# Strided attention on one core: the load of the values as one transfer, or as three on two queues

## The chip, the cores and the metric

The kernel runs on one core of a Trainium2 chip. The metric is the device time of one execution in microseconds (us). Before the change the median of three runs is 127.71 us (127.59 to 128.22).

## What is computed

Q, K and V have the shape 8 x 12 x 1024 x 64 (batch, heads, sequence, dimension) in float32. Each query attends to every 64th key, so to 16 keys per head:

```python
attend_positions = np.arange(0, seq, stride)            # 16 positions
k = K[:, :, attend_positions, :]
v = V[:, :, attend_positions, :]
scores = np.einsum('bhqd,bhkd->bhqk', q, k) * scale
weights = np.exp(scores - np.max(scores, axis=-1, keepdims=True))
weights = weights / (np.sum(weights, axis=-1, keepdims=True) + 1e-10)
result[:, :, i, :] = np.einsum('bhqk,bhkd->bhqd', weights, v)[:, :, 0, :]
```

All of Q is read (25.2 MB) and a result of the same size is written. Of K and of V only 1536 rows of 64 numbers are read, 256 bytes each and far apart, 384 KB for each of the two.

## The kernel before, in words

The 96 heads are worked off in 24 groups of four heads. A group's queries are one load of 1 MB (L33, through the helper `_copy`, on the queue of the SyncE engine), its result is one store of 1 MB on the same queue. There are ten buffers for queries and eight for results.

At the start SyncE issues, in this order: the load of all keys (L106), the query load of group 0, the load of all values (L108), and the query loads of groups 1 to 9. After that, each pass of the loop over the groups issues the store of group g and then the query load of group g + 10, as long as there are groups left. The loads of the first two groups are laid out in 128 rows of 8 KB, the others in 32 rows of 32 KB; a store has rows of 8 KB as far as the DMA engines see it.

The order of the instructions on each engine is written out by hand (`manual_schedule`): every engine works through its list in that order, and waits stand where data are needed.

GpSimd (POOL) begins with the identity matrix (L121, L122), four copies that make `perm_v` from it (L129), and then waits for `s_sel`, which VectorE (DVE) makes from the identity (L136), to fill `v_all` and `mask` (L140, L141). Then come copies of keys into `k_t` (L159), its halves of the casts of the queries of groups 0 and 1 (L196), and the cast of the values to bf16 (`v_bf`, L294), the first instruction that reads the loaded values. Behind `v_bf` TensorE (PE) spreads the values over the partitions (L171), VectorE copies that to `v_rep` (L175), and GpSimd multiplies it with the mask (`v_all`, L184): this is the right side of the matmuls that make the outputs (L255).

Per group: ScalarE (ACT) and GpSimd each cast one half of the queries (L195, L196), VectorE transposes them in 32 x 32 blocks (L212), TensorE makes the scores (L221), ScalarE takes the exponential (L233), TensorE makes the outputs and the sums of weights in three pieces (L255), VectorE takes the reciprocals (L263) and multiplies two of the pieces by them (L265), while the third is copied by ScalarE (L269) and multiplied by GpSimd (L270). Then the group is stored.

Of the kernel before, what the change touches and what calls it, by code (L numbers as in the profile page):

```python
# [17 lines left out]
def _ap_with(ap: bass.AP, new_ap, extra_offset: int = 0) -> bass.AP:  # L18
    return dataclasses.replace(
        ap, ap=[list(p) for p in new_ap], offset=ap.offset + extra_offset  # L20
    )
# [27 lines left out]
def kernel(  # L49
# [8 lines left out]
    nc = tc.nc  # L58

    B, H, S, D = Q.shape  # L60
# [24 lines left out]
    v_raw = const.tile([P, NC, D], FP32, name="v_raw")  # L85
# [5 lines left out]
    kv_src = [[stride * D, P], [2 * HG * SD, NC], [1, D]]  # L91
# [6 lines left out]
    def load(g):  # L98
        qn[g] = qn_bufs[g % QBUFS]
        n = P if g < 2 else 32  # L100
        loaded[g] = _copy(nc, qn[g], _ap_with(Q, [[HG * SD // n, n], [1, HG * SD // n]], g * HG * SD))
        if g >= QBUFS:
            for earlier in (loaded[g - QBUFS], *cast_by[g - QBUFS]):
                implied(loaded[g], earlier, "the store before it has waited for both casts")

    nc.sync.dma_start(k_raw, _ap_with(K, kv_src))  # L106
    load(0)
    nc.sync.dma_start(v_raw, _ap_with(V, kv_src))  # L108
    for g in range(1, QBUFS):
        load(g)  # L110

# [172 lines left out]
    first, rest = slice(0, 4), slice(4, NC)  # L284
# [76 lines left out]
```

## Time and profile before

| what | value |
|---|---|
| median of three runs | 127.71 us (127.59 to 128.22) |
| the profiled execution: its time | 128.23 us |
| its span (first to last instruction) | 126.4 us |
| busy PE / DVE / ACT / POOL | 65.1 / 85.4 / 82.8 / 78.7 us |
| DMA packets, data moved | 7910, 51.19 MB, 405 GB/s over the span |
| of them under 512 B | 3872 |
| load of the values: issue on SyncE, time to landing | 2.00 us, 6.5 us |
| first reader of the values, `v_bf` on POOL | starts at 12.10 us |
| first store issued | 21.21 us |

The page of a profile lists the engines' busy times, the DMA queues with their packets and the share of the time of sixteen DMA engines that these took, and the chain of work that ended last. Other views of the same trace are the table of stretches (busy time of each engine, and share of the DMA engines, between two times), the timeline of one engine, and the waits of one tile. Times in them are microseconds from the start of the span. The trace also records each DMA packet with its queue, size, start and duration, and each mark by which a DMA engine reports its part of a transfer as landed; the records do not name the engine.

A transfer is cut into runs of consecutive bytes, which the trace shows as packets: the keys and the values together are 3072 packets of 256 bytes on SyncE's queue (q1), queries and results are packets of 8 KB and 32 KB. Every transfer of this kernel ends with sixteen marks, one for each DMA engine.

### The profile page before, as it was taken

How to read it: one execution, taken by the hardware profiler on the slowest of the kernel's cores; microseconds unless marked ns; L12 is line 12 of the kernel's file. 1: busy time of each engine (PE TensorE's matmuls, PEld its weight loads, DVE VectorE, ACT ScalarE, POOL GpSimd, SP SyncE). 2: the span in 40 equal slices, each digit the busy share in tenths (PEclk: the TensorE clock that was granted, in tenths of full speed). 3: DMA queues.
4: the chain of work that ended last, by engine and by line, in shares of the span. 5: the costliest groups of instructions: out<-in, count | busy, mean ns of one | idle time of the engine just before them, and what ended most of it. 6: DMA issues, size and time to landing. Idle time of an engine off the chain costs nothing.

```text
span 126.4 us, 1091 instructions
## 1 busy us (share of the span) xinstructions
PE 65.1 (52%) x292; PEld 28.6 (23%) x292; DVE 85.4 (68%) x151; ACT 82.8 (66%) x111; POOL 78.7 (62%) x89
## 2 busy tenths in 40 slices
PE   0005379446666655866666656657794486430000
PEld 0001132212322223333333332212321223200000
DVE  5931672959698979799999998955955956750000
ACT  4172809794989999969898988477486496620000
POOL 4084347763858688969898999566666756453000
PEclk9999999996899998599999999975569959955555
DMA  2999999989998998989989999989989899999991
GB/s 63 381 357 454 487 404 425 498 332 397 438 482 358 482 459 337 513 355 423 474 371 430 461 394 441 477 365 469 435 378 503 345 428 423 428 425 425 425 410 44
DMA packets 7910, 51.19 MB, mean 405 GB/s; under 512 B 3872, under 2 KB 3872, under 8 KB 3872
## 3 DMA queue, kind: packets, MB, share of 16 engines
q1 hardware_dynamic: 7904, 51.12, 96.9%
q8 instruction: 2, 0.03, 0.1%
q14 instruction: 4, 0.03, 0.1%
HBM read 25.95 MB, written 25.17 MB: 404 GB/s over the span
## 4 chain that ended last, share of the span: by engine, by line
DMA 50%; DVE 12%; ACT 10%; POOL 7%; PE 6%; issue 3%; SPq 2%; POOLq 1%; DVEq 0%
DMA qn<-in_Q_dram 50%; DVE out_sb L265 6%; ACT out_sb L269 4%; POOL out_sb L270 4%; PE o_ps L255 3%; DVE qt L212 3%; ACT qb L195 2%; POOL qb L196 2%; ACT w_all L233 2%; PE sc L221 2%; DVE rec L263 2%; ACT k_t L159 1%; POOLq L356 1%; SPq L33 1%; DVE v_rep L175 1%
## 5 line engine op out<-in xcount | busy, mean ns | idle before, releaser
L255 PE MATMUL o_ps<-v_all,w_all 128*128 128x260 bf16 x192 | 37.6, 310 | 35.8 <-DVE out_sb L265 26.1
L270 POOL TENSOR_TENSOR out_sb<-out_sb,rec 128x768 f32<-128x768 f32 x24 | 35.3, 1472 | 19.6 <-ACT out_sb L269 19.1
L265 DVE TENSOR_TENSOR out_sb<-o_ps,rec 128x768 f32<-128x768 f32 (+1 forms) x48 | 39.6, 824 | 1.6
L212 DVE STREAM_TRANSPOSE qt<-qb 128x1024 int32<-128x1024 int32 x24 | 29.4, 1226 | 13.9 <-POOL qb L196 13.9
L233 ACT ACTIVATE w_all<-sc 64x512 bf16<-64x512 f32 x48 | 35.3, 736 | 3.5 <-PE sc L221 3.0
L221 PE MATMUL sc<-qt,k_t 128*128 128x512 bf16 x96 | 32.0, 467 | 9.9 <-DVE qt L212 9.9
L255 PEld LDWEIGHTS <-w_all 128*128 128x128 bf16 x192 | 17.4, 106 | 60.5 <-DVE out_sb L265 33.7
L196 POOL CAST qb<-qn 128x1024 bf16<-128x1024 f32 x24 | 24.9, 1038 | 9.7 <-ACT qb L195 7.8
L195 ACT CAST qb<-qn 128x1024 bf16<-128x1024 f32 x24 | 25.0, 1046 | 8.9 <-DMA qn<-in_Q_dram 8.6
L269 ACT COPY out_sb<-o_ps 128x768 f32<-128x768 f32 x24 | 19.2, 799 | 13.3 <-DVE rec L263 12.9
L263 DVE RECIPROCAL rec<-o_ps 128x12 f32<-128x12 f32 (+1 forms) x72 | 15.1, 209 | 4.2 <-PE o_ps L255 3.7
L184 POOL TENSOR_TENSOR v_all<-mask,v_rep 128x256 bf16<-128x256 bf16 x24 | 16.1, 672 | 1.9 <-DVE v_rep L175 1.9
L221 PEld LDWEIGHTS <-k_t 128*128 128x128 bf16 x96 | 10.8, 113 | 20.2 <-POOL k_t L159 7.5
L159 ACT COPY k_t<-k_r 32x256 bf16<-32x256 bf16 (+1 forms) x12 | 4.4, 366 | 1.5 <-DVE k_r L150 1.3
L175 DVE CAST v_rep<-o_ps 128x768 bf16<-128x768 f32 x2 | 1.9, 956 | 4.4 <-PE o_ps L171 4.4
L133 DVE MEMSET k_t<- 128x3456 uint32 x1 | 2.9, 2938 | 1.5 <-PEq L342 1.5
L149 ACT CAST k_bf<-k_raw 128x256 bf16<-128x256 f32 (+1 forms) x2 | 1.0, 512 | 2.7 <-DMA k_raw<-in_K_dram 2.7
L140 POOL COPY v_all<-s_sel 128x12 bf16<-128x12 bf16 x1 | 0.2, 194 | 4.1 <-DVE s_sel L136 4.1
L171 PE MATMUL o_ps<-v_bf,perm_v 128*128 128x384 bf16 x4 | 1.3, 417 | 1.5 <-POOL v_bf L294 1.2
L149 ACT ACT_TABLE_LOAD x1 | 1.3, 1283 | 0.7 <-PEq L342 0.7
L150 DVE STREAM_TRANSPOSE k_r<-k_bf 128x128 int32<-128x128 int32 (+1 forms) x2 | 0.7, 370 | 1.4 <-ACT k_bf L149 1.4
L134 DVE MEMSET w_all<- 128x1536 uint32 x1 | 1.3, 1338 | 0.3 <-issue 0.3
(12 smaller groups left out, 4.6 us busy)
## 6 DMA issues: line engine op xcount, KB each, us to landing
qn<-in_Q_dram SPq DMA_DIRECT2D x24, 1024.0 KB, 15.3
out_dram<-out_sb SPq DMA_DIRECT2D x24, 1024.0 KB, 15.4
k_raw<-in_K_dram SPq DMA_DIRECT2D x1, 384.0 KB, 4.0
v_raw<-in_V_dram SPq DMA_DIRECT2D x1, 384.0 KB, 6.5
```

Of the source, the lines that this page charges most:

```text
L159: op(k_t[dst : dst + 32, 2 * part.start + c : 2 * part.stop : 2, :, col : col + NK], k_r[src : src + 32, part].rearrange("p n (a k f) -> p ...
L184: masked[g] = nc.gpsimd.tensor_tensor(out=vb[g][:, 0 : 4 * D].rearrange("p (s d) -> p s d", s=4), in0=mask, in1=v_rep[:, g // 2, g % 2].un ...
L195: late = nc.scalar.copy(qb[g][:, half:], qn[g][:, half:])
L196: early = nc.gpsimd.tensor_copy(out=qb[g][:, 0:half], in_=qn[g][:, 0:half])
L212: turned = nc.vector.transpose(qt[g].bitcast(I32), qb[g].bitcast(I32))
L221: nc.tensor.matmul(sc, lhsT=k_t[:, g, f, NK * (1 - e) : NK * (1 - e) + P], rhs=_ap_with(q, [q.ap[0], [D, 8], [16 * D, 2], [2, 32]], extra_ ...
L233: raised[g].append(nc.scalar.activation(out=_ap_with(wa, [wa.ap[0], [P, 8], [1, 2], [2, 32]], extra_offset=64 * a), in_=sc[64 * a : 64 * a ...
L255: nc.tensor.matmul(ps[:, i, 0 : 4 * D + 4], lhsT=wt[g][:, i0 + i], rhs=vb[g], start=True, stop=True,)
L263: nc.vector.reciprocal(r, ps[:, 0:n, 4 * D : 4 * D + 4])
L265: timed = nc.vector.tensor_tensor(out=to, in0=o, in1=by, op=ALU.mult)
L269: copied = nc.scalar.copy(to, o)
L270: scaled[g] = nc.gpsimd.tensor_tensor(out=to, in0=to, in1=by, op=ALU.mult)
```

## The change

The single load of the values (128 rows, one for each partition, each with 12 runs of 256 bytes) becomes three: rows 0 to 4 and rows 5 to 125 on the queue of GpSimd, and rows 126 and 127 on that of SyncE, there in the old place between the first two query loads. The two on GpSimd stand ahead of all its other instructions of the kernel. `v_bf` now waits for three transfers. The order of all other instructions on every engine is as before.

```diff
     nc.sync.dma_start(k_raw, _ap_with(K, kv_src))
     load(0)
-    nc.sync.dma_start(v_raw, _ap_with(V, kv_src))
+    def value_load(queue, first, rows):
+        queue.dma_start(
+            v_raw[first : first + rows],
+            _ap_with(V, [[stride * D, rows], *kv_src[1:]], first * stride * D),
+        )
+
+    value_load(nc.gpsimd, 0, 5)
+    value_load(nc.gpsimd, 5, 121)
+    value_load(nc.sync, 126, 2)
     for g in range(1, QBUFS):
         load(g)
```

## The prediction

> **What bounds the kernel now.** I read the DMA queues first, then the table of stretches, then the timelines of SP and POOL around the transfer that is changed, and last the trace's records of single DMA packets, which no view prints.
>
> The queues, on the page:
>
> ```profile
> q1 hardware_dynamic: 7904, 51.12, 96.9%
> q8 instruction: 2, 0.03, 0.1%
> q14 instruction: 4, 0.03, 0.1%
> HBM read 25.95 MB, written 25.17 MB: 404 GB/s over the span
> ```
>
> Packets, MB, and the share of 16 DMA engines' whole span: SP's queue keeps the sixteen engines busy 96.9% of 126.4 us, while the busiest compute engine has 68%. The table of stretches (columns: stretch, length, busy us and instructions of PE, PEld, DVE, ACT and POOL, PE clock, DMA share, GB/s) says when they are not busy:
>
> ```profile
> 3.00:31.00 28.00, 12.52 (x44) 5.17 (x45) 17.04 (x27) 15.55 (x23) 14.67 (x20) 0.97 1.03 414
> 31.00:50.00 19.00, 11.77 (x61) 5.38 (x60) 16.25 (x30) 18.31 (x28) 14.21 (x14) 0.95 1.01 427
> 75.00:101.00 26.00, 16.73 (x72) 6.87 (x71) 19.37 (x37) 16.95 (x22) 17.79 (x17) 0.80 1.01 426
> 115.00:123.00 8.00, 0.00 (x0) 0.00 (x0) 0.00 (x0) 0.00 (x0) 0.00 (x0) 0.50 1.01 424
> 123.00:124.00 1.00, 0.00 (x0) 0.00 (x0) 0.00 (x0) 0.00 (x0) 0.00 (x0) 0.50 0.36 148
> 124.00:125.00 1.00, 0.00 (x0) 0.00 (x0) 0.00 (x0) 0.00 (x0) 0.00 (x0) 0.50 0.14 57
> ```
>
> From 3 to 123 us all sixteen are full; compute is over by 115. Then the share falls to 0.36 and 0.14: **most engines are done and a few are not**. The sixteen completion marks of the last store show it: ten at 123.44 to 123.80 us, three at 124.03, 124.18 and 124.22, three at 125.09, 125.17 and 125.54. The span ends on the last one. An even share would have ended at about 124.0 (mean of the sixteen), so at most some 1.5 us can be won by sharing the packets out otherwise.
>
> Why are three late? The records carry no engine number, but on a full engine a 256 B packet follows the one before after 14 ns, an 8 KB packet after 307, so most can be strung into sixteen chains. Two of the three last chains lose 1.08 us at 48.0 and 1.01 us at 85.1, just behind the two 16 KB packets of q8 (47.0 and 84.1 us). Chains hit by an 8 KB packet of q14 lose about 0.3 us. The rest are short delays of single packets. So part of the lateness belongs to the engines that fetch instructions, and part is chance.
>
> **The change, part by part.** The time of this execution is 128.23 us: the span of 126.42 and 1.81 around it. The median of the runs shown is 127.71 (127.59 to 128.22), so the profiled one is the slow end, 0.4% above; I carry the ratio over to the median.
>
> *Packets of V per engine.* Before, 128 rows of 12 runs of 256 B on sixteen engines: 96 packets each, from 6.28 to 7.64 us on the first, 1.36 us, or 14 ns a packet. If the change's "5 and 11" holds and the two transfers take different engines, five engines get 1 row (12 packets) and eleven get 11 rows (132). Two engines get another 12 packets for SP's 2 rows; I take them to be among the five, otherwise two of the eleven are 0.17 us later. The five save 84 x 14 ns = **1.18 us** (1.01 with the extra row), the eleven pay 36 x 14 ns = **0.50 us**. All transfers behind V on an engine move by as much, since every engine is full from there to 123 us. Total work is unchanged. Completion marks cost 9 ns each: nothing.
>
> *The sum, if the three late engines are among the five:* the last goes from 125.54 to 124.36 (or 124.53), and what is late next are the eleven: the latest of the others, 124.22 + 0.50 = 124.72. The end moves by 125.54 - 124.72 = 0.82: 128.23 - 0.82 = 127.41 us, -0.64%, which on the median is **126.9**. With fewer hiccups among the eleven (123.80 + 0.50 = 124.30; then the end is the 124.53 of above) it is -1.01, 126.7; with a hiccup of 0.3 us (such as a q14 fetch) on one of them, -0.5, 127.2.
>
> *Issue on SP.* Three things of SP's start are touched:
>
> ```profile
> 0.74 0.43 SPq L106 DMA_DIRECT2D k_raw<-in_K_dram  x1
> 1.23 0.73 SPq L33 DMA_DIRECT2D qn<-in_Q_dram  x1
> 2.00 0.58 SPq L108 DMA_DIRECT2D v_raw<-in_V_dram  x1
> 21.21 0.63 SPq L33 DMA_DIRECT2D out_dram<-out_sb  x1
> 27.95 0.59 SPq L33 DMA_DIRECT2D out_dram<-out_sb  x1
> 33.18 0.59 SPq L33 DMA_DIRECT2D out_dram<-out_sb  x1
> ```
>
> The 2-row transfer keeps an issue slot between the first and second Q load: 0.43 to 0.73 us by these rows instead of 0.58, hidden behind 2.4 us of packets per load already queued. First data come 1.1 us after the K issue starts, at 1.84 us, and K stays first: no change.
>
> *Issue on POOL.* Two issues go ahead of everything POOL does:
>
> ```profile
> 0.73 0.21 POOL L121 MEMSET identity<- 128x128 bf16 x1 [0.29 <-POOLq L342]
> 1.01 0.29 POOL L122 TENSOR_SCALAR_AFFINE_SELECT identity<-identity 128x128 bf16<-128x128 bf16 x1
> 1.37 0.76 POOL L129 COPY perm_v<-identity 128x64 bf16<-128x64 bf16 x4
> 6.28 0.19 POOL L140 COPY v_all<-s_sel 128x12 bf16<-128x12 bf16 x1 [4.15 <-DVE s_sel L136]
> ```
>
> No row shows what an issue costs on POOL. Behind the two wait the identity (DVE's s_sel at 5.99 needs it, ready at 1.30: 4.7 us to spare), perm_v, and then the 4.15 us in which POOL waits anyway. Call the cost of both G. Lower bound: as SP, 2 x 0.43 = 0.9 us. Upper bound, if GpSimd writes 1512 runs one by one at the pace of its slowest row per element (L270, 1472 ns for 768): 2.9 us for one list, 5.8 if sources and destinations are two lists done in turn. I take 3, nearer to the one list. Up to 4.15 it is free.
>
> *Arrival of V.* L294 needs all three transfers; behind it on POOL are both value products, and behind those the first outputs. It runs at 12.10 while V has landed at 8.5: 3.6 us to spare. And the start as a whole has cover: store 0 is issued at 21.21, its data could flow at 22.3, but the engines are on the ten first Q loads until 30.2. Stores 1 and 2 have 6.0 and 5.6 us by the same count. So the delay D of the first outputs costs nothing up to 5.6 us (V landing by 17.7, or G up to 9.7), and D - 5.6 beyond.
>
> **A rule against it.** The trace prices V by which engines carry it, not by its total. The Trainium skill ("DMA: Bandwidth & Descriptors", section "Rules for kernel authors") says of two transfers to disjoint partition halves not to bother: they spread over the same sixteen engines, and one 128-partition transfer is to be used. By that rule the sum would be zero, 127.7.
>
> **The rivals.**
> *B, the late engines are not the five.* The trace does not show which engines the 5 rows fall on. If the last one is among the eleven it ends at 125.54 + 0.50: 128.73, or 128.2 on the median, +0.4%. For it: lateness is partly chance, and eleven of sixteen engines pay. Against: two of the three follow instruction fetches, so the same engines would be late each time.
> *C, the split isn't what it says.* If the 121 rows go to all sixteen engines in eights, each has 96 packets again, give or take a row (0.17 us): 127.7 (127.5 to 127.9). Then no engine takes much over 96 runs in the after trace. The Trainium skill (same page, section "Why a DMA increments its semaphore by 16 and not by 1") has both: the largest divisor up to 16, so 5 and 11, and an exception in which some direct GpSimd copies get sixteen engines with the rows rounded up. No trace here shows which.
> *D, V comes late.* On an engine, packets of another queue are taken between packets of a store (the fetches above do so in the middle of one). If the 132 runs of V take turns singly with Q's packets, they get 16 turns beside the 8 KB packets of the first two loads (5.1 us) and 16 beside the 32 KB packets of the other eight (1.23 us each, 19.8 us), and finish when those run out, at about 30. Then L294 waits 18 us more, D - 5.6 = 12.6, and the time is 140.8 in the profile's count (140 on the median). If sixteen runs go at a turn, 9 turns at most 1.45 us each end by 17, and it costs nothing. It decides at 17.7 us. A G of over 9.7 us has the same effect; at 12 us it costs 2.3.
>
> **How the numbers follow.** A 0.53 (126.3 to 127.3; a twentieth of the total within 0.5%), B 0.14 (mostly within), C 0.09 (within), D 0.24 (128.5 to 141, of it 0.07 up to 129; not more in all, since 9.7 lies above my upper bound for G, and turns of single runs are the extreme). A difference of 0.5%, 0.64 us, is about what a measurement of this kernel can tell from none. Faster 0.48, same 0.25, slower 0.27. The range 126.2 to 129.0 takes in A, B, C and the small cases of D; left out are the rest of D (0.17) and a little below (0.03).
>
> **What would show it.** Right: the sixteen marks of the last store lie closer, with the end set by an engine with 132 V packets; the DMA share in the second before last is higher; span near 125.6. Step by step: chains with 12 and 132 runs of 256 B besides K's; L294 before 17.7 us; store 2 issued before 38.8; no drop of the DMA share near 30 us. A stretch near 30 to 40 us with a share under 0.9 means D; marks as wide as before with all 0.5 later means B.

## The result, and the profile after

The changed kernel takes **130.21 us** (median of six runs, 130.00 to 130.36) where the kernel before takes 127.96 (127.59 to 128.35, six runs beside it): a ratio of 1.0175 (1.0149 to 1.0200), 2.25 us slower. The forecast was 126.9 us; the time lies above the range. The profiled execution took 130.16 us with a span of 128.3, to be set against 128.23 and 126.4 before.

The queues of the changed kernel, from the page:

```profile
q1 hardware_dynamic: 6378, 50.73, 95.4%
q0 software_dynamic: 192, 0.39, 1.1%
q8 instruction: 2, 0.03, 0.1%
q14 instruction: 5, 0.03, 0.1%
HBM read 25.95 MB, written 25.17 MB: 398 GB/s over the span
```

The bytes are the same and go at 398 GB/s instead of 404. The new queue q0 is GpSimd's. Its 192 packets are taken apart below. The table of stretches, cut as in the prediction and with the start cut finer (columns as there):

```profile
3.00:7.00 4.00, 0.00 (x0) 0.00 (x0) 3.16 (x4) 0.93 (x3) 2.30 (x10) 1.00 0.99 288
7.00:9.50 2.50, 0.00 (x0) 0.10 (x1) 0.00 (x0) 0.07 (x1) 0.45 (x2) 1.00 1.06 354
```

```profile
31.00:50.00 19.00, 11.13 (x55) 5.32 (x56) 16.95 (x32) 16.74 (x26) 13.32 (x14) 0.91 1.00 423
75.00:101.00 26.00, 15.38 (x79) 7.04 (x78) 20.81 (x39) 20.23 (x26) 19.83 (x20) 0.94 1.00 422
```

```profile
124.00:125.00 1.00, 0.00 (x0) 0.00 (x0) 0.00 (x0) 0.00 (x0) 0.00 (x0) 0.50 0.90 377
125.00:126.00 1.00, 0.00 (x0) 0.00 (x0) 0.00 (x0) 0.00 (x0) 0.00 (x0) 0.50 0.35 147
126.00:127.00 1.00, 0.00 (x0) 0.00 (x0) 0.00 (x0) 0.00 (x0) 0.00 (x0) 0.50 0.14 57
```

At the end the same falling stair stands as before, 0.35 and 0.14, only two us later: the engines are no more level than they were. From 31 to 101 us the engines are as full as before and move about as much. At the start, though, the share stays at 0.99 and 1.06 while 288 and 354 GB/s are moved. The same two stretches in the kernel before:

```profile
3.00:7.00 4.00, 0.00 (x0) 0.00 (x0) 3.16 (x4) 0.93 (x3) 0.66 (x3) 1.00 1.04 351
7.00:9.50 2.50, 0.00 (x0) 0.10 (x1) 0.87 (x1) 1.70 (x4) 2.06 (x5) 1.00 1.18 394
```

**The engines are occupied there without moving data at their usual pace.** That is a loss that a share of busy time does not show and the last column does.

The completion marks of each load and store, one for each engine, place it (median of the sixteen, in us; the last column is the time from the load of group 9 to the end, the stretch in which nothing was changed). The times of loads are the ends of the marks' packets, those of the end are the marks' arrivals, some 0.4 us later in every trace; the last column has this difference in all rows:

| kernel | load 0 | load 2 | load 0 to load 2 | load 9 | end: first, median, last | load 9 to end |
|---|---|---|---|---|---|---|
| before | 6.60 | 12.97 | 6.38 | 30.05 | 123.44, 123.74, 125.54 | 93.69 |
| after | 7.43 | 14.84 | 7.41 | 31.89 | 125.06, 125.57, 127.24 | 93.68 |

The end is 1.83 us later on the median engine and 1.70 on the last one. Of it 0.83 is there by load 0 and another 1.03 by load 2, which is where the values are carried; from then on both kernels need the same time. Of the sixteen marks of load 2, four lie at 14.39 to 14.52, eleven at 14.70 to 15.18 and one at 16.61. The step that I priced at -1.18 us on five engines and +0.50 on eleven **made all sixteen later**: the first mark of load 2, at 14.39, comes 1.3 us behind the last one of before (13.07). One engine lost more than the others: its load 0 ends at 9.56, the other fifteen by 7.79. It keeps this distance and is one of the two that end last, at 127.17 and 127.24.

The timelines of SP and POOL show that the rest went much as worked out. SP, after:

```profile
0.74 0.46 SPq L106 DMA_DIRECT2D k_raw<-in_K_dram  x1
1.26 0.72 SPq L33 DMA_DIRECT2D qn<-in_Q_dram  x1
2.02 0.50 SPq L109 DMA_DIRECT2D v_raw<-in_V_dram  x1
...
25.02 0.63 SPq L33 DMA_DIRECT2D out_dram<-out_sb  x1
...
31.75 0.59 SPq L33 DMA_DIRECT2D out_dram<-out_sb  x1
...
36.98 0.59 SPq L33 DMA_DIRECT2D out_dram<-out_sb  x1
```

POOL, after:

```profile
1.37 2.01 POOL L109 DMA_DIRECT2D v_raw<-in_V_dram  x2 [0.92 <-POOLq L350]
3.37 0.22 POOL L129 MEMSET identity<- 128x128 bf16 x1
...
6.28 0.19 POOL L148 COPY v_all<-s_sel 128x12 bf16<-128x12 bf16 x1 [1.50 <-DVE s_sel L144]
...
14.78 1.03 POOL L204 CAST qb<-qn 128x1024 bf16<-128x1024 f32 x1 [2.74 <-DMA qn<-in_Q_dram]
15.90 0.83 POOL L302 CAST v_bf<-v_raw 128x768 bf16<-128x768 f32 x1
```

The two issues on GpSimd take 2.01 us together, and the next instruction with a fixed date, `v_all` behind `s_sel`, starts at 6.28 as before: the issue cost is free. `v_bf` starts at 15.90 instead of 12.10. The page's list of transfers (KB, median us from issue to landing) has the 121 rows landing 13.7 us after their issue, so at about 15.8:

```profile
v_raw<-in_V_dram POOLq DMA_DIRECT2D x1, 363.0 KB, 13.7
v_raw<-in_V_dram POOLq DMA_DIRECT2D x1, 15.0 KB, 4.5
```

The first store is issued 3.81 us later (25.02), the second 3.80, the third 3.80.

**What the 192 packets of q0 are.** The packet records by size:

```
88 of 4096 B + 11 of 1024 B = 11 engines x (8 x 16 + 4) runs  = 132 runs of 256 B each
 5 of 3072 B                =  5 engines x 12 runs            =  12 runs of 256 B each
40 of 64 B + 5 of 16 B      =  5 engines x (8 x 16 + 4) runs  = 132 runs of 4 B each
11 of 48 B                  = 11 engines x 12 runs            =  12 runs of 4 B each
32 of 4 B                   =  2 transfers x 16 marks
```

The first two lines are the split that the change names, 11 and 5. The third and fourth are work that nobody asked for: for each of the two transfers, the engines that have no row get as many runs as the others, of 4 bytes each. (The records name no engine: that the small runs lie on the engines without rows is read from the counts. Nor do they say whether the 5 and the 11 are different engines; the sum does not depend on it.) So every engine has 144 runs on q0, where it had 96 on SP's queue before.

### The profile page after: what moved, and what is told of

Its sections match the earlier page's. It is cut to its first block, busy times and chain, and to the rows that moved or that the text cites. A ratio compares the mean times of both kernels' runs of the same rounds, so it can differ in the third digit from the quotient of the medians.

```text
span 128.3 us, 1095 instructions
## 1 busy us (share of the span) xinstructions
PE 64.0 (50%) x292; PEld 28.7 (22%) x292; DVE 85.1 (66%) x151; ACT 82.8 (64%) x111; POOL 80.6 (63%) x91
## 4 chain that ended last, share of the span: by engine, by line
DMA 39%; DVE 18%; ACT 12%; PE 9%; POOL 8%; issue 3%; SPq 2%; POOLq 1%; DVEq 0%
DMA qn<-in_Q_dram 39%; DVE out_sb L273 9%; PE o_ps L263 5%; DVE qt L220 5%; ACT out_sb L277 4%; PE sc L229 4%; POOL out_sb L278 3%; ACT qb L203 3%; POOL qb L204 3%; DVE rec L271 3%; ACT w_all L241 2%; ACT k_t L167 2%; POOLq L364 1%; SPq L33 1%; DVE v_rep L183 1%
## 5 line engine op out<-in xcount | busy, mean ns | idle before, releaser
L263 PE MATMUL o_ps<-v_all,w_all 128*128 128x260 bf16 x192 | 37.1, 307 | 35.9 <-DVE out_sb L273 26.7
L109 POOL DMA_DIRECT2D v_raw<-in_V_dram x2 | 2.0, 1007 | 0.9 <-POOLq L350 0.9
## 6 DMA issues: line engine op xcount, KB each, us to landing
v_raw<-in_V_dram POOLq DMA_DIRECT2D x1, 363.0 KB, 13.7
```

The costliest lines, as they stand in the source:

```text
L263: nc.tensor.matmul(ps[:, i, 0 : 4 * D + 4], lhsT=wt[g][:, i0 + i], rhs=vb[g], start=True, stop=True,)
```

## The experiments

Two suspicions come out of this. *Empty engines*: what counts on an engine is runs and not bytes, and a GpSimd transfer with fewer rows than engines gives every engine the same number of runs; 144 instead of 96 explain the 1.03 us. *First transfer*: the 0.83 us ahead of load 0 come from the small GpSimd transfer that is the first of its queue. The rivals are that runs cost more on GpSimd's queue than on SP's, that the eleven engines with 132 runs were the late ones all along (rival B of the prediction), and that the later outputs cost something after all. The rows of a table like the above are given once, behind the experiments. The runs came in four sets, and each set shares its runs of the kernel before, with medians of 128.08, 128.15, 128.05 and 128.19 us.

### One transfer on GpSimd

```diff
-    nc.sync.dma_start(v_raw, _ap_with(V, kv_src))
+    nc.gpsimd.dma_start(v_raw, _ap_with(V, kv_src))
```

> The values in one transfer of 128 rows on GpSimd's queue: 96 runs of 256 B on each of sixteen engines, no unequal shares and no engine left out. Theory 1 (GpSimd's runs are dearer for every DMA engine: 18 ns each instead of 14, the engines that carry no data get as many small runs of 4 B at nearly the same price, and the first use stalls all engines for some 0.65 us): 96 x 4 to 6 ns + 0.65, so about 1.1 us slower than before, half of what the three transfers cost. Theory 2 (the values come late and the first outputs with them): L294 would again run some 3 us late and cost about 2 us. Theory 3 (only the unequal shares cost): 0.

128.07 us, ratio 1.0003 (0.9985 to 1.0021): no difference. The queue, on its page:

```profile
q0 software_dynamic: 112, 0.39, 1.0%
```

These are 96 packets of 4096 B, six for each engine, and 16 marks: no runs of 4 B. Load 0 to load 2 takes 6.23 us, no more than before. With 96 runs on each engine in both kernels, GpSimd's runs are not dearer than SyncE's.

### The same three pieces, all on SyncE

```diff
-    value_load(nc.gpsimd, 0, 5)
-    value_load(nc.gpsimd, 5, 121)
+    value_load(nc.sync, 0, 5)
+    value_load(nc.sync, 5, 121)
     value_load(nc.sync, 126, 2)
```

> The same three transfers, 5, 121 and 2 rows, all on SyncE's queue. Theory 1: nothing of GpSimd's price remains; what remains is how the 256 B packets are shared out, up to 156 on the most loaded engine instead of 96 (60 x 14 ns = 0.84 us): between -0.5 us (the late engines are ones that now carry nothing) and +0.85 us (they are the most loaded). Theory 2: the values land under 1 us later than before, 0. Theory 3 (the shares cost): about as slow as the three transfers on two queues, +2.2 us.

130.89 us, ratio 1.0228 (1.0178 to 1.0279): as slow as the change, by another way. SP's timeline:

```profile
2.01 5.19 SPq L109 DMA_DIRECT2D v_raw<-in_V_dram  x3
7.24 5.64 SPq L33 DMA_DIRECT2D qn<-in_Q_dram  x9
```

The three issues take 0.53, 0.29 and 4.28 us. The third stands in SP's instruction stream until 7.2, and with it the nine query loads behind it, of which the first was issued at 2.63 before. Part of the engines run dry; in this stretch the kernel before has a share of 1.18 and 394 GB/s:

```profile
7.00:9.50 2.50, 0.00 (x0) 0.10 (x1) 0.88 (x1) 1.69 (x4) 2.05 (x5) 1.00 0.91 184
```

So this kernel can't say what the 5 and 11 shares are worth without empty engines, which is what I sent it for. It has no packets on q0, and its three pieces end in 5, 11 and 2 marks, where each transfer of GpSimd ends in 16.

### More work for five engines alone, on SyncE and on GpSimd

Both kernels are the one before with 5 rows of 84 runs of 256 B more, in three transfers into result buffers that are not yet in use. Nothing reads them.

```diff
+    for i in range(3):
+        nc.sync.dma_start(
+            out_bufs[OBUFS - 1 - i]...[0:5, 0 : 28 * D]...,
+            _ap_with(V, [[stride * D, 5], [SD, 28], [1, D]]),
+        )
```

behind the ten query loads in the one, and the same with `nc.gpsimd`, ahead of GpSimd's cast for group 2, in the other.

> Which engines are late? The kernel before, and behind the ten first query loads three more transfers on SyncE's queue, of 5 rows with 28 runs of 256 B each, into buffers not yet in use: 84 packets more, 1.2 us, on five engines only. If the engines that end last are among the five that such a transfer uses, the end moves by about 1.2 us; if they are among the others, by 0 to 0.3 us (the five would have to overtake the late ones). The trace says for each of the five where it ends.

SyncE: 129.89 us, ratio 1.0145 (1.0114 to 1.0176). The end marks part: five at 126.06, 126.16, 126.28, 126.48, 126.91, the other eleven at 123.46 to 124.97. Before, the three late ones were at 125.09, 125.17 and 125.54; with 84 x 14 ns = 1.18 us they would be at 126.27, 126.35 and 126.72, so it is tempting to find them among the five. But the five are late already at the first store, right behind the three transfers: five marks at 34.10 to 35.16, eleven at 32.40 to 33.18. The two groups can be followed from there, transfer by transfer. Behind each of the two 16 KB packets of q8 (at 47.1 and 87.4 us) one mark leaves the group of eleven and stays some 1.4 us behind it; these two end at 124.95 and 124.97. One of the five loses half a microsecond behind the last 8 KB packet of q14 (114.7 us), as the third late engine of the kernel before does behind its own (116.4 us). In the kernel before two of the three late engines, the last one included, were late behind q8. **If q8 falls on the same engines in every execution, these two are among the eleven and only the third among the five: that speaks for rival B.** It isn't settled, since no record names an engine and the five that GpSimd's transfer uses need not be SyncE's five.

> As the run with three more transfers of 5 rows with 28 runs of 256 B, but on GpSimd's queue, issued behind the values' products. Theory A (engines without rows get a small run for every run that the others get, at nearly the same price): all sixteen engines lose 84 x 16 ns = 1.3 us or more, the marks of the last store of the eleven as well, and the packets show 84 runs of 4 B on each of eleven engines. Theory B (engines without rows are spared): the eleven end where they end in the run on SyncE's queue (123.6 to 125.0 us), give or take the first use (0.5 us), and only five end late.

GpSimd: 130.03 us, ratio 1.0168 (1.0128 to 1.0208). The queue:

```profile
q0 software_dynamic: 144, 0.11, 0.3%
```

144 packets are 3 x 16 marks, 30 with the 420 runs asked for, and 66 of 64 and 48 B: in each transfer 28 runs of 4 B on each of the eleven engines without a row. Whichever five each transfer uses, all sixteen engines have 84 runs more, and all sixteen pay for them. The first eleven of the end marks lie at 124.51 to 125.36, where the first eleven were at 123.46 to 124.97 in the kernel on SyncE and at 123.44 to 124.03 before: the first of all is 1.1 us later than in either. Load 9 ends at 31.20 instead of 30.05. That is 1.1 to 1.2 us for 84 runs, **13 to 14 ns for a run of 4 bytes, about what a run of 256 bytes costs** (14). The packets' own durations do not show this price: a packet of 16 such runs is recorded with 25 ns (median), one of 4096 B with 174. A fixed loss of 0.4 us for each small transfer would look the same; against it speaks the kernel below with one transfer of 5 rows issued at 2.08 us, which lost nothing. (The last mark, at 127.71, belongs to an engine that fell some 3 us behind during the three transfers; why is open.)

### GpSimd transfers with and without empty engines

```diff
+    value_load(nc.gpsimd, 0, 16)
+    value_load(nc.gpsimd, 16, 112)
```

> The values in two transfers on GpSimd's queue as in the change, but of 16 and 112 rows, which sixteen divides: every engine has 12 and 84 runs, none is left out. Theory A (the price is that of transfers that leave engines out: those get small runs of 4 B at nearly full price, and the others' runs cost 20 ns): as the single transfer of 128 rows on GpSimd, 0 to +0.5 us against before. Theory B (every transfer on GpSimd's queue costs a stall of its own, 0.6 us): +1.2 us. Theory C (the unequal shares alone): 0.

Two transfers of 16 and 112 rows use all sixteen engines: 129.51 us, ratio 1.0120 (1.0072 to 1.0169). Its 144 packets on q0 are 112 with data and 32 marks, none of 4 B. Load 0 to load 2 takes 6.30 us: the 1.03 us are gone. But load 0 is 1.13 us late. The small transfer alone costs this, with no empty engine in it.

```diff
+    value_load(nc.gpsimd, 0, 121)
+    value_load(nc.sync, 121, 7)
```

> One transfer of 121 rows on GpSimd's queue and 7 rows on SyncE's; the transfer of 5 rows is gone. Theory A: the dear part of the change is still there, 132 runs at 18 to 20 ns on eleven engines and as many of 4 B on five: +1.3 to +2 us. Theory B: one stall, +0.6 us. Theory C: eleven engines have 36 packets more, some of them 12 more from SyncE: +0.5 to +0.7 us.

One GpSimd transfer of 121 rows, the rest on SP: 129.06 us, ratio 1.0090 (1.0055 to 1.0125). Here load 0 is on time (6.69) and load 0 to load 2 takes 7.14 us, 0.76 more than before, with 40 packets of 64 B and 5 of 16 B. All sixteen marks of load 2 lie within 13.49 to 14.23, those of the five engines without rows too. This is the other half of the loss by itself.

```diff
+    value_load(nc.gpsimd, 0, 120)
+    value_load(nc.sync, 120, 8)
```

> 120 rows on GpSimd's queue, which fifteen divides, 8 rows on SyncE's: fifteen engines have 96 runs as before, one has none but small ones. Theory A in the form that small runs on the left-out engines are what costs: only one engine has them and it saves its 96 packets, so about 0 to +0.5 us. Theory A in the form that runs are dear as soon as sixteen doesn't divide the rows: 96 x 6 ns and the first use, +0.8 to +1.2 us. Theory B: +0.6 us. Theory C: 0.

120 rows go to fifteen engines and leave one empty (6 packets of 64 B): 129.20 us, ratio 1.0078 (1.0046 to 1.0110), with runs from 128.33 to 131.73. Load 0 to load 2 takes 6.65. With 96 runs on each engine the theory has no more than the 8 rows on SP to add (0.17 us); it measured 0.27. Its packets of 4096 B last 210 ns by the median, those of the change 205 and those of the single 128-row transfer 159; but the means are 214, 202 and 219, so it isn't shown that packets are slower where an engine is empty.

### The small transfer first, or not

```diff
-    value_load(nc.gpsimd, 0, 5)
     value_load(nc.gpsimd, 5, 121)
+    value_load(nc.gpsimd, 0, 5)
```

> The changed kernel with its two transfers on GpSimd in the other order: 121 rows first, then 5. Theory A (a small first transfer reaches the engines early, between the keys and the first queries, and stalls all of them for 0.6 to 0.8 us; a large first one does not): the marks of the first query load come at 6.2 to 7.1 us again, and of the 2.25 us of the change some 0.7 us go away, 129.4 us. Theory B (each transfer on GpSimd's queue costs a stall, in whatever order): no different from the change, 130.2 us. Theory C (what counts is that the late engines carry the few rows): now eleven engines from the first on have the 121 rows, the late five among them, so slower than the change by up to 1 us.

The change with its two GpSimd transfers swapped: 129.52 us, ratio 1.0120 (1.0082 to 1.0159), 0.7 us less than the change. Load 0 is at 6.67 and load 0 to load 2 takes 7.52 us: the first loss is gone and the second is whole. The two add up.

```diff
+    nc.gpsimd.dma_start(spare[0:5, 0 : NC * D]..., _ap_with(V, [[stride * D, 5], *kv_src[1:]]))
```

> The kernel before, with its one transfer of the values on SyncE, and in addition GpSimd loads the first 5 rows once more into an output buffer that is not yet in use: the first use of GpSimd's queue alone, with 12 runs a row. Theory 1: the first use costs all engines about 0.65 us and the runs 0.2: +0.8 us. Theory 2: nothing that the first outputs need is later by more than 1 us: 0. Theory 3: five engines get 12 packets more, 0.17 us at most: 0 to +0.2.

The kernel before with the five rows loaded once more by GpSimd, ahead of all else, into a buffer that nothing reads yet: 128.64 us, ratio 1.0046 (1.0012 to 1.0080). Load 0 comes at 7.22 (+0.62), and nothing is lost behind it (6.24). A transfer of 15 KB delays every engine by 0.6 us. One engine's load 0 ends at 8.10.

> The first use alone (5 rows more on GpSimd's queue, into a buffer not yet in use), also issued behind perm_v. Theory A1: only its 12 runs are left, 0.2 us: 128.2 us, no difference that can be told. Theory A2: +0.5 us as ahead of the identity, 128.6 us.

The same five rows, issued behind `perm_v` (at 2.08 us instead of 1.35): 128.39 us, ratio 1.0013 (0.9992 to 1.0034). Load 0 is at 6.40: nothing.

> The changed kernel with its two transfers on GpSimd issued behind perm_v instead of ahead of the identity, some 1 us later; their order is the change's, 5 rows first. Theory A1 (the stall of some 0.7 us on all engines comes because the first transfer arrives between the keys and the first queries, at 3.8 to 4.6 us): the marks of the first query load are back at 6.2 to 7.1 us and the time is that of the swapped order, 129.5 us. Theory A2 (a small transfer that is the first on GpSimd's queue stalls the engines whenever it arrives): the marks behind it come 0.6 to 0.8 us late again, and the time is the change's, 130.2 us.

The change with both GpSimd issues behind `perm_v`: 130.74 us, ratio 1.0184 (1.0131 to 1.0237), the runs at 130.09, 130.15, 131.33 and 132.86. Load 0 is at 6.94, so the first loss is 0.34 instead of 0.83; load 0 to load 2 takes 7.42. The median engine ends 0.27 us sooner than in the change and the last one at 127.27, as there, and the last one sets the time. The delay of load 0 thus shrinks when the small transfer comes 0.7 us later, but no time is won. POOL's row:

```profile
2.08 2.01 POOL L109 DMA_DIRECT2D v_raw<-in_V_dram  x2
```

> All 128 rows in one transfer on GpSimd's queue, issued behind perm_v. Issued first it took as long as the kernel before, with one engine 1.2 us behind the others from the first query load on. If that engine is held up by the early arrival, it no longer is, and the last engine ends up to 0.6 us earlier: 127.5 to 128.0 us. If it is the first use as such, 128.0 to 128.3 us.

All 128 rows on GpSimd, behind `perm_v`: 128.24 us beside 128.19, ratio 1.0000 (0.9984 to 1.0016). Neither loss is there (6.58; 6.30).

### The outputs later

Both kernels are the one before with extra work on POOL ahead of the cast of the values, which makes the first outputs late and leaves the loads alone.

```diff
+    for _ in range(4):
+        nc.gpsimd.tensor_copy(out=spare[:, 0 : 16 * D], in_=qn[1][:, 0 : 16 * D])
```

> The kernel before, with four copies of 128 x 1024 on GpSimd ahead of L294, some 4 us, so that the values' cast and all first outputs are as late as in the changed kernel (store 0 at about 25 us) while the DMA transfers are those of before. Theory 1: 0, the ten first query loads cover it until 30 us. Theory 2: the same loss as the change, +2.2 us. Theory 3: 0.

129.82 us, ratio 1.0085 (1.0046 to 1.0125). The first store is issued at 25.49, 4.28 us late. The prediction had this free up to 5.6. The runs spread from 128.35 to 131.05, and the profiled one is the highest, so I went on to a cleaner form of it:

```diff
+    for _ in range(5):
+        nc.gpsimd.tensor_copy(out=v_bf, in_=k_raw)
```

> The first outputs late by some 4 us once more, now by five casts of the keys into the tile that the values' cast then overwrites, so that no buffer of queries or results is touched. If lateness up to 5.6 us is covered by the query loads in the queue: 0 (within 0.4%). If lateness itself costs, as the run with four copies suggests: +1.1 us again.

131.09 us, ratio 1.0209 (1.0154 to 1.0265). Its stores on SP:

```profile
25.96 0.62 SPq L33 DMA_DIRECT2D out_dram<-out_sb  x1
...
32.69 0.59 SPq L33 DMA_DIRECT2D out_dram<-out_sb  x1
...
37.73 0.59 SPq L33 DMA_DIRECT2D out_dram<-out_sb  x1
```

They are 4.75 us late. The engines do not fall idle:

```profile
31.00:50.00 19.00, 11.19 (x60) 5.07 (x59) 16.75 (x31) 17.27 (x27) 14.01 (x13) 0.94 1.04 400
```

The share is 1.04, and 400 GB/s go through instead of 427. The packets of this stretch last longer: those of 32 KB 1.39 us on the mean instead of 1.22, those of 8 KB 330 ns instead of 312. Stores 1 to 3 are issued 1.85 to 3.27 us ahead of the time at which the engines reach them (store 2 in the kernel before: 6.7 us, in the change: 4.7, because the loads ahead of it are late as well). So lateness can cost before the engines run dry, from a delay of about 4 us on; the runs of the first of the two kernels reach from next to no loss (128.35) to 3 us. Why the packets last longer is open. In the change itself there is none of it: 311.8 ns and 1.22 us, and load 9 to end 93.68.

### The idea without the values

```diff
+    query_rows(nc.gpsimd, 0, 5)
+    query_rows(nc.gpsimd, 5, 121)
```

> The idea of the change with few and long runs: the values are loaded as before; half of the query load of group 9 (4 KB of each of 128 rows, needed only some 40 us later) is loaded as 5 and 121 rows on GpSimd's queue, issued behind perm_v, and 2 rows on SyncE's. The five engines save 7 x 4 KB (1.05 us; two of them 0.9), eleven carry 3 x 4 KB more (0.46 us), and the small runs are only 12 for each engine. Theory A (the late engines are the first five; runs are dear because they are many; the first use costs about 0.5 us): 0.8 to 1.0 us gained, 0.5 lost: -0.5 to 0 against before. Theory B (any use of GpSimd's queue with 5 and 121 rows costs what it cost in the change): +1 to +2 us.

Here the values are loaded as before, and half of the query load of group 9 (rows of 4 KB) is split 5, 121 and 2, so that uneven shares come with few runs. 128.89 us, ratio 1.0070 (1.0042 to 1.0097), the runs from 128.40 to 131.58: no gain. I have no trace of it that can be compared with the others, so why it loses is open. No kernel of this study beat the one before.

### The marks of all of them

| kernel | median, us | profiled run, us | load 0 | load 0 to load 2 | load 9 to end |
|---|---|---|---|---|---|
| before | 127.96 | 128.23 | 6.60 | 6.38 | 93.69 |
| after | 130.21 | 130.16 | 7.43 | 7.41 | 93.68 |
| 121 first, then 5 | 129.52 | 129.49 | 6.67 | 7.52 | 93.74 |
| 5, 121 behind `perm_v` | 130.74 | 130.15 | 6.94 | 7.42 | 93.87 |
| 121 on GpSimd, 7 on SyncE | 129.06 | 129.06 | 6.69 | 7.14 | 93.85 |
| 120 on GpSimd, 8 on SyncE | 129.20 | 128.72 | 6.81 | 6.65 | 93.74 |
| 16, 112 on GpSimd | 129.51 | 130.36 | 7.73 | 6.30 | 93.75 |
| 128 on GpSimd | 128.07 | 128.92 | 6.57 | 6.23 | 93.67 |
| 128 on GpSimd behind `perm_v` | 128.24 | 128.04 | 6.58 | 6.30 | 93.74 |
| before and 5 rows first | 128.64 | 129.51 | 7.22 | 6.24 | 93.72 |
| before and 5 rows behind `perm_v` | 128.39 | 128.19 | 6.40 | 6.36 | 93.73 |
| outputs 4.75 us late | 131.09 | 130.96 | 6.41 | 6.24 | 94.99 |

The marks are those of the profiled run, which was well above the median for 16 and 112 rows, for 128 rows and for 5 rows first. Read by columns: load 0 to load 2 is long in just the rows that have engines without a row in a large GpSimd transfer (7.14 to 7.52, and 6.65 with one such engine), whatever else they do. Load 0 is over 7.2 in just the rows whose first GpSimd transfer is small and issued at 1.31 to 1.37 us.

## Why the prediction was wrong, step by step

**The step that failed** is the packets of V per engine: "The five save 84 x 14 ns = 1.18 us (1.01 with the extra row), the eleven pay 36 x 14 ns = 0.50 us", and with it "Total work is unchanged". The count of *real* runs was right for each transfer, 12 and 132. But the engines without rows were given 132 and 12 runs of 4 B besides, so all sixteen had 144 in place of 96, total work in runs grew by half, and there was no short share to win with. By my own price, 48 x 14 ns = 0.67 us is what this costs every engine. Of it 12 runs, 0.17 us, fall to the time ahead of load 0, since the packets of the small transfer start at 3.76 to 4.84 us. The stretch from load 0 to load 2 thus has 36 runs more, 0.50 us, and 1.03 was measured there; what the other half is stays open. That the engines without rows are not spared is shown by the counts, by the price of 84 small runs in the kernel with 5 rows more on GpSimd, and by the marks of load 2, all sixteen of which are late after the change and with 121 rows on GpSimd alone.

**What was missing** is a price for the start of the small transfer. I costed GpSimd's issue on POOL and the arrival of V, and took the DMA engines' side of the first transfer at nothing. It cost 0.83 us on the median engine. The five rows alone, early, cost 0.62, and with the large transfer first 0.7 us of the time came back: that the small, early transfer delays load 0 is shown. In the change the five packets of 3072 B lasted 732 ns (median), and packets of 8 KB that were under way at 3.9 to 5.2 us up to 1.97 us; with the large transfer first the five lasted 135. What it is in this first transfer that holds all sixteen engines up isn't settled: issued 0.7 us later it does nothing alone, and 0.34 us in the change.

**The sum** from the runs: 0.83 + 1.03 - 0.03 (load 2 to load 9: 17.05 us after, 17.08 before) - 0.01 behind it = 1.82, and the median engine ends 1.83 later; the medians of the time are 2.25 apart, the two profiled executions 1.93.

**The idea of the gain** was not put to the test, and what it rests on isn't shown. I took the three late engines to be among the five. In the kernel with 5 rows more on SyncE the two engines behind q8 are among the eleven and only the third late one is among the five, so for the engine that ended last before the change rival B is the likelier reading. The split that should relieve five engines relieves none on this queue, and on SyncE's queue, where 5 rows do go to 5 engines alone, SP stood for 4.28 us. The sign that I gave for rival B, marks as wide as before and all later, is just what came (2.18 us wide after, 2.10 before), but the runs of 4 B bring it about too. A sign that two causes share should not have been given to one.

**Rival C**, a split that isn't 5 and 11, is false for the rows and true in effect: the engines were loaded alike. Its price of nothing was wrong, since the even load is the dearer one.

**Rival D**, V coming too late, did not happen: `v_bf` started at 15.90, ahead of 17.7, and store 2 was issued at 36.98, ahead of 38.8. But my cover of 5.6 us was too generous. I counted until the engines would run dry; kernels with outputs 4.28 and 4.75 us late lost 1.1 and 2.7 us by their ratios (0.85% and 2.09%), the second with its engines full. The change, 3.81 us late and with its loads late as well, stayed just clear of that.

**G**, the issue on POOL, came out at 2.01 us, against 3 taken and bounds of 0.9 and 5.8, and free as said. The 2-row issue on SP, 0.50 us against 0.43 to 0.73, as said.

**The rule against the change** was on the right side. The Trainium skill ("DMA: Bandwidth & Descriptors", section "Rules for kernel authors") says of two transfers to disjoint partition halves not to bother and to use one 128-partition transfer; I gave it a time of no change. Here one 128-row transfer is as good on either queue (128.07 and 128.24 beside 128.08 and 128.19), and the pieces cost between 0.9 and 2.8 us: the trace agrees with the rule and adds that the split is not merely idle.

The range failed because every case in it shared one premise, that runs which nobody asked for do not exist, and none had a price for the start of a small transfer. The lower chance that I gave to slower (0.27) came from V's lateness alone.

## What to carry to other kernels

Before you steer load between DMA engines with the number of rows of a transfer, count in the trace what each engine really gets, small packets too: on GpSimd's queue the engines without rows got a run of 4 bytes for each run of the others, at nearly the same price. Where a busy share stays at 1 and the time grows, read the bytes per second beside it and the marks stage by stage; the stage that grows names the cause sooner than the end of the span does. And a piece that is cut off a transfer has a price of its own at its issue and at its start, which the sum over bytes or runs does not hold.

## What the runs showed of the hardware that was not expected

- By the counts of its packets, a GpSimd transfer of 121 rows in 12 runs ran on eleven engines with real data and on five with as many runs of 4 B; 120 rows used fifteen and one, 5 rows five and eleven. Each ended in 16 marks. Three transfers that gave every engine 84 runs, of 4 B where it had no row, made load 9 some 1.1 us later. On SyncE's queue transfers of 5, 121 and 2 rows ended in 5, 11 and 2 marks.
- GpSimd's queue shows sixteen runs of 256 B as one packet of 4096 B (159 ns in the best case), SyncE's one packet for each run; for 96 runs the engines needed as long on the one as on the other (6.23 and 6.38 us from load 0 to load 2).
- A first GpSimd transfer of 15 KB, issued at 1.35 us beside full engines, delayed load 0 by 0.62 us on the median engine, and nothing when issued at 2.08.
- Of three issues in a row on SP (5, 121 and 2 rows) the third stood 4.28 us, where the others took 0.53 and 0.29.
- With the stores issued only 1.85 to 3.27 us ahead of their turn, packets grew (32 KB: 1.39 us on the mean instead of 1.22) while the share of the engines stayed at 1.04.
